# Attention: eight modulation blocks from TensorE to VectorE, loads in another order, results of two head pairs kept in h

## The chip, the cores and the metric

One core of a Trainium2 chip. The metric is the device time of one execution in microseconds (us). Engines are named as in the profile: PE (TensorE matmul), PEld (TensorE weight load), DVE (VectorE), ACT (ScalarE), POOL (GpSimd), SP (SyncE, which here only issues DMAs).

## The reference, cut to what matters

```python
def modulate(h, shift, scale):
    return h * (1 + scale) + shift
...
        sm, cm, gm, sf, cf, gf = adaln(c, w_ada[l], b_ada[l])    # silu(c) @ w_ada + b_ada, in six parts
        h = modulate(rmsnorm(x, norm_mix_g[l]), sm, cm)
            q, k, v = qkv_proj(h, w_qkv[j])
            o = neighbourhood_attention(q, k, v, cache_k[:, j], cache_v[:, j], rpb[j])
            mix = merge_heads(o) @ w_attn_out[j]
        x = x + gm * mix
        h = modulate(rmsnorm(x, norm_ffn_g[l]), sf, cf)
        x = x + gf * conv_ffn(h, ...)
```

Two layers, 1024 features, 16 heads of 64, 128 prompt tokens (conditioned by c_ctx) and 256 sample tokens (conditioned by c). Layer 0 mixes by attention, layer 1 by a gated MLP over chunks. In attention a prompt token sees the 128 prompt keys; a sample token sees the 256 sample keys within a window of columns, with a learned bias, and 128 cached keys. Everything is float32.

## The kernel before

Activations lie feature-major: x[k] holds 128 features of all 384 tokens. A float32 product is three products in a faster format, of operands split into a high part and a rest: hi·hi, hi·lo, lo·hi (`mac`, L101 to L105). Splitting a weight takes a cast on ACT (`hi`) and a subtraction on DVE (`lo`), L108 and L109. Weights come as tiles of 128 x 1024 (512 KB).

Attention (`attention`, L388) first makes V for all heads, then runs over eight pairs of heads (L597), with the keys of the next pair and the queries of the next pair made inside the pair; then come eight output products, one for each 128 features (`output`, L638), each followed by `residual` (L374). From L580 on the four engines PE, ACT, DVE and SP issue in the order in which the code is written (`tc.manual_schedule`); each engine runs its own list in order. What a pair's weights go through: `fetch` (L445) has SP load the next one into one of three buffers `st`; `ready` splits the oldest staged one and then calls `fetch`, so SP's next load waits until `lo` has read its buffer. `hi` and `lo` have five buffers each.

A pair t in the code before, in its order: scores of the sample's first 128 queries (and the prompt's); SP's loads of the next pair's cached keys (`cache`, tile kT) and bias (`bias_load`, two loads into btr); bias, minimum and exponentials (`exps`, L522: a DVE reduction that also adds the bias, then ACT's exponentials with their sums); transposes of the last pair's first head (`turn`); division by the sums (`normalized`, L540); the key product of the next pair; a `ready` (the *first lo*); scores of the second 128 queries; `keys` (khi on ACT, klo on DVE); `exps`, `turn`, `normalized` for them; the query product, a `ready` (the *second lo*), `bias`, `queries`, `values` of the last pair, and three steps of `ada`.

The modulations come from two places. `Ada` (L160) does blocks on PE: a block is 128 rows of w_ada for one of the parts gm, sf, cf of layer 0 (24 blocks, 512 KB each, buffers adw, four of them), L190; three are loaded and three are run in each pair. `AdaV` (L222) does the rest (56 blocks) on DVE in later stages: a block is 128 outputs of one part, multiplied by silu(c) and silu(c_ctx) (tiles cs, laid out over all partitions), each in one instruction that sums along the row (L248), and then the bias is added (L250).

Of the kernel before, what the change touches and what calls it, by code (L numbers as in the profile page):

```python
# [8 lines left out]
F32 = mybir.dt.float32  # L9
# [6 lines left out]
P = 128  # L16
D = 1024
# [22 lines left out]
def backbone(ctx: ExitStack, tc: tile.TileContext, xT_in, cond_in, condr_in, b_ada_in, prm_in,  # L40
# [17 lines left out]
    def bank(pool):  # L58
        return pool.tile([P, 512], F32, name="bank", tag="bank")
# [47 lines left out]
    def split(hi, lo, src):  # L107
        nc.scalar.copy(hi, src)  # L108
        nc.vector.tensor_tensor(lo, src, hi.bitcast(F32), ALU.subtract)  # L109
# [50 lines left out]
    class Ada:  # L160
# [1 line left out]


        def __init__(self):
            order = [(0, GM), (0, SF), (0, CF)]
            self.todo = [(l, pc, k) for l, pc in order for k in range(KD)]
            self.ready = []
            self.pa = self.done = None
# [9 lines left out]

        def run(self, n):
            for _ in range(n):  # L180
                if not self.ready:
                    self.load(1)
                self.one(*self.ready.pop(0))

        def one(self, l, pc, k, t):
            self.flush()
            if k == 0:
                self.pa = bank(ps_ad)
            for j in range(4):
                nc.tensor.matmul(self.pa[32 * j:32 * j + 32, 0:256], cond_s[:, k, :],  # L190
                                 t[:, 256 * j:256 * j + 256], start=(k == 0),
                                 stop=(k == KD - 1), tile_position=(0, 32 * j))
# [25 lines left out]
    class AdaV:  # L218


        def __init__(self):
            self.cs = self.junk = None  # L222

            def both(l, p, q):
                return [(l, pc, k) for k in range(KD) for pc in (p, q)]

            def one(l, p):
                return [(l, p, k) for k in range(KD)]

            self.todo = (both(1, SM, CM)[:8]  # L230
                         + [t for k in range(KD) for t in ((0, GF, k), both(1, SM, CM)[8 + k])]
                         + one(1, GM) + both(1, SF, CF) + one(1, GF))

        def start(self, pool):
            self.cs = [pool.tile([P, D], F32, name=f"cs{c}") for c in range(2)]
            self.junk = pool.tile([P, D], BF16, name="junk")
# [4 lines left out]
        def run(self, n):  # L241
            for _ in range(n):
                l, pc, k = self.todo.pop(0)
                t = adp.tile([P, D], F32, name="adw", tag="adw")
                nc.sync.dma_start(t, w_adaT[l, pc, k])
                m = mods[l][:, pc, k]
                for c in range(2):
                    tc.keep_in_program_order(nc.vector.tensor_tensor_reduce(  # L248
                        self.junk, t, self.cs[c], 1.0, 0.0, ALU.mult, ALU.add, m[:, c:c + 1]))
                nc.vector.tensor_scalar(m, m, b_ada[:, l, pc * 8 + k:pc * 8 + k + 1], None, ALU.add)  # L250
                if pc in (CM, CF):
                    gain(l, pc, slice(k, k + 1))

    ada_v = AdaV()

# [6 lines left out]
    def square(k, tag="t384", apart=True):  # L262

        sq["last"] = None
        if k == 0:
            sq["acc"] = tmp.tile([P, NT], F32, name="sqacc", tag="sqacc")
            nc.scalar.activation(sq["acc"], x[k], AF.Square)
            return
        t = tmp.tile([P, NT], F32, name="t384", tag=tag, bufs=2 if tag == "t384" else 1)
# [78 lines left out]
    def norm_first(nxt, units):  # L348

        w = [load(u) for u in units]  # L350
        Rp = rms()
        R = tmp.tile([P, NT], F32, name="R0", tag="R0")
# [35 lines left out]
    def attention(pool, wkp):  # L388
# [13 lines left out]
        ohi = [pool.tile([P, NT], F32R, name=f"ohi{t}") for t in range(NPAIR)]  # L402
        olo = [pool.tile([P, NT], F32R, name=f"olo{t}") for t in range(NPAIR)]
# [6 lines left out]
        R = tmp.tile([P, NT], F32, name="R0", tag="R0")  # L410
# [11 lines left out]
        for b in range(3):  # L422
            for half in range(2):
                nc.scalar.copy(V[:, b, 512 * half:512 * half + 512], acc[3 * half + b])
        nc.gpsimd.dma_start(sv_out, V[:, 0, :])

        allm = slice(0, P)

# [37 lines left out]
            return p  # L466

        def cache(t):
            kT = wkp.tile([P, 512], F32, name="kT", tag="kT", bufs=1)
            nc.sync.dma_start(kT[:, 256:384], ckT_in[:, t, :])  # L470
            return kT

        def keys(t, kT, p):
            nc.scalar.copy(kT[:, 0:256], p[:, 0:256])
            nc.scalar.copy(kT[:, 384:512], p[:, 256:384])  # L475
            nc.gpsimd.dma_start(skT_out[:, t, :], kT[:, 0:NPR])
            k = [wkp.tile([P, 512], F32R, name=n, tag=n) for n in ("khi", "klo")]
            split(*k, kT)
            return k

        def queries(p):
# [77 lines left out]
            nc.scalar.copy(pT[:, 512:896], two[1][:, :384])  # L559
            return pT  # L560

        def values(t, pT, pool=ps_mm):


            pv = bank(pool)
# [17 lines left out]
        for _ in range(3):  # L583
            fetch()
        kT, btr = cache(0), bias_load(0)
        nc.sync.dma_start(cv, cv_in)
        ada.load(3)
        ready()
        p = products()
        ready()  # L590
# [2 lines left out]
        ready()  # L593
        bias(btr)
        Q = queries(p)
        old = None
        for t in range(NPAIR):  # L597
            last = t == NPAIR - 1
# [17 lines left out]
            if last:  # L616
                ada.run(3)
            else:
# [5 lines left out]
            if not last:  # L624
                p = products()
                ready()
                bias(btr)
                Q = queries(p)
                if old is not None:
                    values(t - 1, pT)  # L630
                ada.run(3)
                ada.load(3)
                old = [(pr[hh], pc[hh]) for hh in range(2)]


        out = {}
# [17 lines left out]
        ready()  # L654
# [9 lines left out]
        for m in range(4, KD):  # L664
            output(m, range(KD), ps_mm if m % 2 else ps_sc)
            if m < KD - 2:
                ready()
            residual(0, GM, m, out[m][1], (0, SF, CF))


# [142 lines left out]
            residual(1, GM, m, ps, (1, SF, CF))  # L813


    with tc.tile_pool(name="att", bufs=1) as pool, tc.tile_pool(name="attw", bufs=2) as wkp:
        attention(pool, wkp)
    csp = ctx.enter_context(tc.tile_pool(name="cs", bufs=1))
    ada_v.start(csp)
# [97 lines left out]
```

## Time and profile before

| what | value |
|---|---|
| median of 3 runs | 1020.77 us (1020.12 to 1022.55) |
| profiled execution, time | 1021.07 us |
| its span | 1019.3 us |
| PE busy | 997.6 us (98%) |
| PEld busy | 947.1 us (93%) |
| DVE busy | 775.9 us (76%) |
| ACT busy | 482.0 us (47%) |
| DMA queue of SP (q1) | 170.11 MB, 51.8% of 16 engines |

The eight pairs take the stretch from about 74 to 190 us of the span, the output products end at 232 us, and the rest is the feed-forward and gated stages. In the profile's rows, "out<-in" names the tiles an instruction writes and reads, xN is a count, and an arrow to a releaser names what ended a wait. A busy engine's share is a mean over all stages.

### The profile page before, as it was taken

Reading aid. Unit: us, or ns where it says so; the run is one execution under the profiler, and the core shown is the slowest. Engines: PE = TensorE matmul, PEld = TensorE weight load, DVE = VectorE, ACT = ScalarE, POOL = GpSimd, SP = SyncE. Lnnn points to the kernel's source line nnn. Section 1 sums busy time; section 2 is a strip of 40 time slices with the busy share of each in tenths; the row PEclk is TensorE's granted clock in tenths of the full one; section 3 lists DMA queues with packets and bytes.
Section 4 is the critical chain, followed back from the end, with each engine's and each line's share of the span. In section 5 each row is a group of like instructions: output and inputs, shape, how many; then the busy total and the mean of one; then the engine's idle time right before and its main releaser. Section 6 shows DMA issues by size and latency. Waiting matters only on the chain.

```text
span 1019.3 us, 15937 instructions
## 1 busy us (share of the span) xinstructions
PE 997.6 (98%) x6012; PEld 947.1 (93%) x6012; DVE 775.9 (76%) x1591; ACT 482.0 (47%) x841; POOL 14.7 (1%) x29
## 2 busy tenths in 40 slices
PE   7999999999999999999999999999999999999996
PEld 6788788789999999999998889999999999999996
DVE  3646666568999898999989999688598777776652
ACT  3446555557655555433354434343385444443331
POOL 1000000000000000000000000000000000000000
PEclk7999999999999999999999999999999999999998
DMA  7874646624465555576737765565325434435521
GB/s 261 303 251 147 211 153 220 230 83 146 136 191 169 165 147 159 149 240 203 227 116 258 240 210 154 172 206 187 104 84 166 144 124 125 124 114 172 159 72 62
DMA packets 53933, 172.96 MB, mean 170 GB/s; under 512 B 6225, under 2 KB 12513, under 8 KB 53857
## 3 DMA queue, kind: packets, MB, share of 16 engines
q1 hardware_dynamic: 52992, 170.11, 51.8%
q8 instruction: 47, 0.77, 0.3%
q0 software_dynamic: 432, 1.06, 0.3%
q10 hardware_dynamic: 432, 0.79, 0.2%
q14 instruction: 30, 0.24, 0.1%
HBM read 169.31 MB, written 2.62 MB: 169 GB/s over the span
## 4 chain that ended last, share of the span: by engine, by line
PE 91%; DMA 3%; DVE 2%; ACT 2%; issue 1%; POOL 0%; SPq 0%; POOLq 0%; ACTq 0%; DVEq 0%
PE bank L103 28%; PE bank L105 28%; PE bank L104 28%; DMA kT<-in_ckT 2%; PE bank L145 1%; PE bank L788 1%; PE bank L568 1%; PE bank L519 1%; PE bank L190 1%; PE bank L551 1%; DMA adw<-in_w_ada 1%; PE bank L284 1%; ACT pr L536 0%; DMA cond<-in_cond 0%; PE bank L302 0%
## 5 line engine op out<-in xcount | busy, mean ns | idle before, releaser
L96 ACT CAST hi<-st 128x1024 fp32r<-128x1024 f32 (+1 forms) x192 | 198.1, 1033 | 300.6 <-PE bank L104 239.0
L105 PE MATMUL bank<-hhi,lo 128*128 128x384 f32 (+1 forms) x960 | 325.2, 339 | 0.2 <-DVE lo L109 0.2
L104 PE MATMUL bank<-hlo,hi 128*128 128x384 f32 (+1 forms) x960 | 324.7, 338 | 0.0
L103 PE MATMUL bank<-hhi,hi 128*128 128x384 f32 (+1 forms) x960 | 324.6, 338 | 0.0
L97 DVE TENSOR_TENSOR lo<-st,hi 128x1024 fp32r<-128x1024 f32 (+1 forms) x192 | 230.0, 1199 | 66.4 <-ACT hi L96 66.1
L105 PEld LDWEIGHTS bank<-hhi,lo 128*128 128x128 f32 x960 | 181.1, 189 | 0.5 <-DVE lo L109 0.5
L103 PEld LDWEIGHTS bank<-hhi,hi 128*128 128x128 f32 x960 | 181.0, 189 | 0.4 <-ACT kT L475 0.2
L104 PEld LDWEIGHTS bank<-hlo,hi 128*128 128x128 f32 x960 | 180.4, 188 | 0.1
L248 DVE CUSTOM_DVE_ANT_0 junk<-adw,cs 128x1024 bf16<-128x1024 f32 x112 | 136.6, 1219 | 1.0
L105 PE MATMUL bank<-ahi,lo 128*128 128x384 f32 x352 | 118.9, 338 | 0.0
L104 PE MATMUL bank<-alo,hi 128*128 128x384 f32 x352 | 118.9, 338 | 0.0
L103 PE MATMUL bank<-ahi,hi 128*128 128x384 f32 x352 | 118.7, 338 | 0.0
L105 PEld LDWEIGHTS bank<-ahi,lo 128*128 128x128 f32 x352 | 66.1, 188 | 0.0
L104 PEld LDWEIGHTS bank<-alo,hi 128*128 128x128 f32 x352 | 66.1, 188 | 0.0
L103 PEld LDWEIGHTS bank<-ahi,hi 128*128 128x128 f32 x352 | 66.1, 188 | 0.0
L103 PE MATMUL bank<-hi,hhi 128*128 128x512 f32 x144 | 58.2, 408 | 1.8 <-ACT hhi L330 1.8
L104 PE MATMUL bank<-lo,hhi 128*128 128x512 f32 x144 | 57.4, 398 | 0.0
L105 PE MATMUL bank<-hi,hlo 128*128 128x512 f32 x144 | 57.3, 399 | 0.0
L376 DVE SCALAR_TENSOR_TENSOR x<-bank,mod,x 128x128 f32<-128x128 f32 x64 | 23.8, 412 | 34.4 <-PE bank L105 34.2
L103 PE MATMUL bank<-mhi,hi 128*128 128x384 f32 x128 | 43.3, 339 | 0.0
L105 PE MATMUL bank<-mhi,lo 128*128 128x384 f32 x128 | 43.2, 337 | 0.0
L104 PE MATMUL bank<-mlo,hi 128*128 128x384 f32 x128 | 43.1, 337 | 0.0
(154 smaller groups left out, 1265.5 us busy)
## 6 DMA issues: line engine op xcount, KB each, us to landing
st<-in_w_up SPq DMA_DIRECT2D x88, 512.0 KB, 3.6
adw<-in_w_adaT SPq DMA_DIRECT2D x56, 512.0 KB, 4.2
adw<-in_w_ada SPq DMA_DIRECT2D x40, 512.0 KB, 5.6
st<-in_w_down SPq DMA_DIRECT2D x32, 512.0 KB, 3.6
st<-in_w_qk SPq DMA_DIRECT2D x16, 512.0 KB, 3.7
st<-in_w_gu SPq DMA_DIRECT2D x16, 512.0 KB, 4.3
st<-in_w_gv SPq DMA_DIRECT2D x16, 512.0 KB, 4.5
st<-in_w_gout SPq DMA_DIRECT2D x16, 512.0 KB, 4.5
```

The source lines that it names most:

```text
L96: nc.scalar.copy(hi[:, :n], st[:, :n])
L97: nc.vector.tensor_tensor(lo[:, :n], st[:, :n], hi[:, :n].bitcast(F32), ALU.subtract)
L103: nc.tensor.matmul(out, a[0], b[0], start=start, stop=False)
L104: nc.tensor.matmul(out, a[0], b[1], start=False, stop=False)
L105: nc.tensor.matmul(out, a[1], b[0], start=False, stop=stop)
L145: nc.tensor.matmul(pa[32 * j:32 * j + 32, 0:P], cond_s[:, 4 * hf + kk, :], w[hf][:, kk, P * q:P * q + P], start=(kk == 0), stop=(kk == 3), ...
L190: nc.tensor.matmul(self.pa[32 * j:32 * j + 32, 0:256], cond_s[:, k, :], t[:, 256 * j:256 * j + 256], start=(k == 0), stop=(k == KD - 1), t ...
L248: tc.keep_in_program_order(nc.vector.tensor_tensor_reduce(self.junk, t, self.cs[c], 1.0, 0.0, ALU.mult, ALU.add, m[:, c:c + 1]))
L284: mm = nc.tensor.matmul(ss[:, 2 * b:2 * b + 2], src[:, b * P:(b + 1) * P], ones[:, 0:2], start=(i == 0 and b == 0), stop=(i == len(srcs) - ...
L376: nc.vector.scalar_tensor_tensor(x[m][:, a:b], ps[:, a:b], mod(l, gate, m, c), x[m][:, a:b], ALU.mult, ALU.add)
L519: nc.tensor.matmul(sc[hh][:, cols], q[qp][HS[hh], qs:qs + P], k[kp][HS[hh], ks], start=i == 0, stop=i == 2)
L551: nc.tensor.transpose((ta[:, o:o + P] if g < 2 else tb[:, o - 512:o - 512 + P]), pr[:, b, g * P:g * P + P], ident)
```

## The change

What it does, by parts:

- The eight blocks of gm move from `Ada` to `AdaV`, first in its list. In the attention loop `AdaV`'s step is cut in three: `load` (SP), `half(0)` for the prompt, `half(1)` for the sample and the bias. One block is done in each pair. `Ada` keeps 16 blocks: two are run ahead of the loop and two in each pair up to the seventh.
- cs is loaded and silu taken ahead of the pairs, no longer after attention; the throw-away output of the sums lies in a buffer of tmp during attention.
- The loads of cached keys and bias are issued at the end of a pair, for the pair after the next, ahead of the blocks.
- Cached keys go to a tile of their own (ck), and the keys are split in three pieces from ck and from the product's bank, without the copy to kT; a copy for the output state (sk) is made afterwards.
- `bias` comes ahead of the second `normalized`.
- The results ohi, olo of pairs 6 and 7 lie in columns of hhi and hlo, which hold h until the last query product.
- The end: the last pair stops after its second `exps`; the order of outputs, `values` 6 and 7, transposes and residuals changes, whole outputs 3 to 7 go to five banks, and residuals come three outputs later.

On SP, in the middle of the loop, the loads before (st: weights, adw<-in_w_ada: blocks for PE, kT: cached keys, btr: bias):

```order
L450 DMA st<-in_w_qk 128x1024 x2
L176 DMA adw<-in_w_ada 128x1024 x3
L470 DMA kT<-in_ckT 128x128
L499 DMA btr<-in_rpb 64x2x219 x2
L450 DMA st<-in_w_o 128x1024 x2
```

and now (adw<-in_w_adaT: the block for DVE, ck: cached keys):

```order
L458 DMA st<-in_w_qk 128x1024 x2
L478 DMA ck<-in_ckT 128x128
L509 DMA btr<-in_rpb 64x2x219 x2
L241 DMA adw<-in_w_adaT 128x1024
L176 DMA adw<-in_w_ada 128x1024 x2
L458 DMA st<-in_w_o 128x1024 x2
```

Of the two weights in a row, the first is let go by the first lo and the second by the second lo. Keys and bias moved ahead of the blocks, DVE's block stands behind them, and one block for PE is gone.

On DVE in the same pairs, from the reductions of the first half to the second lo, before:

```order
L533 TENSOR_REDUCE st<-bank 128x1 x2
L541 RECIPROCAL st<-st 128x4
L543 TENSOR_SCALAR pr<-pr,st 128x384 x2
L543 TENSOR_SCALAR pc<-pc,st 128x128 x2
L109 TENSOR_TENSOR lo<-st,hi 128x1024
L109 TENSOR_TENSOR klo<-kT,khi 128x512
L526 ISA bank,st<-bank,bt 128x384
...
L541 RECIPROCAL st<-st 128x2
L543 TENSOR_SCALAR pr<-pr,st 128x384 x2
L109 TENSOR_TENSOR lo<-st,hi 128x1024
L509 TENSOR_TENSOR bt<-mask,btr 128x3x128 x2
L485 SCALAR_TENSOR_TENSOR qlo<-bank,qhi 128x384
```

and now (L246 is the half of a block, L249 its bias):

```order
L543 TENSOR_REDUCE st<-bank 128x1 x2
L246 ISA junk,mod_143<-adw,cs_718 128x1024
...
L551 RECIPROCAL st<-st 128x4
...
L109 TENSOR_TENSOR lo<-st,hi 128x1024
L109 TENSOR_TENSOR klo<-ck,khi 128x128
L109 TENSOR_TENSOR klo<-bank,khi 128x256
...
L519 TENSOR_TENSOR bt<-mask,btr 128x3x128 x2
L551 RECIPROCAL st<-st 128x2
L553 TENSOR_SCALAR pr<-pr,st 128x384 x2
L246 ISA junk,mod_143<-adw,cs_719 128x1024
...
L249 TENSOR_SCALAR mod_143<-mod_143,b_ada 128x2
L109 TENSOR_TENSOR lo<-st,hi 128x1024
```

Half 0 went between the reductions and the first reciprocal, half 1 between the second division and the second lo, the bias moved up, and klo became three pieces (two are shown).

On PE in the last pair, after the second scores, before (ohi: results of pairs as left operand, one row of three shown for a product):

```order
L519 MATMUL bank<-khi,qlo 128x384 x2
L190 MATMUL bank<-adw,cond_s 32x256 x12
L551 MATMUL bank<-ident,pr 128x128 x6
L553 MATMUL bank<-ident,pc 128x128
L103 MATMUL bank<-ohi_177,hi 128x384
```

and now:

```order
L529 MATMUL bank<-khi,qlo 128x384 x2
L103 MATMUL bank<-ohi_180,hi 128x384
...
L103 MATMUL bank<-ohi_185,hi 128x384
...
L561 MATMUL bank<-ident,pr 128x128 x6
L563 MATMUL bank<-ident,pc 128x128
```

The three blocks are gone, and the first output product over pairs 0 to 5 stands ahead of the transposes.

The diff, cut:

```diff
@@ class Ada
-            order = [(0, GM), (0, SF), (0, CF)]
+            order = [(0, SF), (0, CF)]
@@ class AdaV
-            self.todo = (both(1, SM, CM)[:8]
+            self.todo = (one(0, GM) + both(1, SM, CM)[:8]
...
+        def load(self):
+            l, pc, k = self.todo.pop(0)
+            t = adp.tile([P, D], F32, name="adw", tag="adw")
+            nc.sync.dma_start(t, w_adaT[l, pc, k])
+            return l, pc, k, t
+
+        def half(self, c, l, pc, k, t):
+            m = mods[l][:, pc, k]
+            tc.keep_in_program_order(nc.vector.tensor_tensor_reduce(
+                self.junk, t, self.cs[c], 1.0, 0.0, ALU.mult, ALU.add, m[:, c:c + 1]))
+            if c:
                 nc.vector.tensor_scalar(m, m, b_ada[:, l, pc * 8 + k:pc * 8 + k + 1], None, ALU.add)
@@ attention
+        ohi = [pool.tile([P, NT], F32R, name=f"ohi{t}") for t in range(6)] + [hhi[:, t, :NT] for t in (6, 7)]
+        olo = [pool.tile([P, NT], F32R, name=f"olo{t}") for t in range(6)] + [hlo[:, t, :NT] for t in (6, 7)]
...
+        ada_v.start(csp, tmp.tile([P, D], BF16, name="junk", tag="R0"))
...
-            nc.scalar.copy(kT[:, 0:256], p[:, 0:256])
-            nc.scalar.copy(kT[:, 384:512], p[:, 256:384])
             k = [wkp.tile([P, 512], F32R, name=n, tag=n) for n in ("khi", "klo")]
-            split(*k, kT)
+            for o, src in ((256, ck), (0, p[:, 0:256]), (384, p[:, 256:384])):
+                s = slice(o, o + src.shape[1])
+                split(k[0][:, s], k[1][:, s], src)
...
         kT, btr = cache(0), bias_load(0)
+        ada.load(2)
+        block = ada_v.load()
         nc.sync.dma_start(cv, cv_in)
-        ada.load(3)
...
+        kT, btr = cache(1), bias_load(1)
+        ada.run(2)
+        ada.load(2)
         old = None
         for t in range(NPAIR):
...
-            if not last:
-                kT, btr = cache(t + 1), bias_load(t + 1)
             e = exps(0, sc, pr, pc)
+            ada_v.half(0, *block)
...
             e = exps(1, sc, pr, pc)
+            if last:
+                break
             if old is not None:
                 pT.append(turned(1, turn(*old[1])))
+            bias(btr)
             normalized(*e)
+            ada_v.half(1, *block)
+            p = products()
+            ready()
+            Q = queries(p)
+            ada.flush()
+            if old is not None:
+                values(t - 1, pT)
+            if t < NPAIR - 2:
+                kT, btr = cache(t + 2), bias_load(t + 2)
+            ada.run(2)
+            block = ada_v.load()
+            ada.load(2)
...
         output(0, range(6), ps_mm)
+        pT.append(turned(1, turn(*old[1])))
+        normalized(*e)
         ready()
-        values(6, pT, ps_sc)
+        pv = bank(ps_sc)
         output(1, range(6), ps_sc)
+        ada.flush()
+        values(6, pT, pv)
         ready()
+        ada_v.half(1, *block)
         pT = [turned(0, turn(pr[0], pc[0]))]
         output(0, (6,))
         output(1, (6,))
         pT.append(turned(1, turn(pr[1], pc[1])))
-        output(2, range(7), ps_mm)
-        ready()
+        output(2, range(5), ps_mm)
         values(7, pT)
-        output(3, range(7), ps_sc)
-        ada.flush()
-        for m in range(4):
+        output(2, (5, 6))
+        for m in range(3):
             output(m, (7,))
-            residual(0, GM, m, out[m][1], (0, SF, CF))
-            if m == 1:
+        for m in range(3, KD):
+            output(m, range(KD), (ps_sc, ps_ta, ps_ad, ps_mm, ps_sc)[m - 3])
+            if m < KD - 1:
                 ready()
+            residual(0, GM, m - 3, out[m - 3][1], (0, SF, CF))
         order.__exit__(None, None, None)
```

More of the change, by code (lines that the diff above doesn't have):

```diff
@@ L180, in run @@
             for _ in range(n):
-                if not self.ready:
-                    self.load(1)
                 self.one(*self.ready.pop(0))
         def one(self, l, pc, k, t):
-            self.flush()
             if k == 0:
@@ L228, in one, with start @@
                 return [(l, p, k) for k in range(KD)]
-            self.todo = (both(1, SM, CM)[:8]
+            self.todo = (one(0, GM) + both(1, SM, CM)[:8]
                          + [t for k in range(KD) for t in ((0, GF, k), both(1, SM, CM)[8 + k])]
                          + one(1, GM) + both(1, SF, CF) + one(1, GF))
-        def start(self, pool):
+        def start(self, pool, junk):
+            self.junk = junk
             self.cs = [pool.tile([P, D], F32, name=f"cs{c}") for c in range(2)]
-            self.junk = pool.tile([P, D], BF16, name="junk")
             for c in range(2):
@@ L239, in start @@
                 nc.scalar.activation(self.cs[c], self.cs[c], AF.Silu)
[L241 to L249, printed above, removed]
+        def load(self):
[8 more added lines that the diff above has]
+            if c:
                 nc.vector.tensor_scalar(m, m, b_ada[:, l, pc * 8 + k:pc * 8 + k + 1], None, ALU.add)
@@ L252, in run @@
                     gain(l, pc, slice(k, k + 1))
+        def run(self, n):
+            for _ in range(n):
+                block = self.load()
+                for c in range(2):
+                    self.half(c, *block)
     ada_v = AdaV()
@@ L268, in square @@
             return
-        t = tmp.tile([P, NT], F32, name="t384", tag=tag, bufs=2 if tag == "t384" else 1)
+        t = tmp.tile([P, NT if tag == "t384" else 512], F32, name="t384", tag=tag,
+                     bufs=2 if tag == "t384" else 1)[:, :NT]
         nc.scalar.activation(t, x[k], AF.Square)
@@ L351, in norm_first @@
         Rp = rms()
-        R = tmp.tile([P, NT], F32, name="R0", tag="R0")
+        R = tmp.tile([P, 512], F32, name="R0", tag="R0")[:, :NT]
         nc.scalar.copy(R, Rp[:, :NT])
@@ L401, in attention @@
         cv = pool.tile([P, D], F32, name="cv")
-        ohi = [pool.tile([P, NT], F32R, name=f"ohi{t}") for t in range(NPAIR)]
-        olo = [pool.tile([P, NT], F32R, name=f"olo{t}") for t in range(NPAIR)]
+        ohi = [pool.tile([P, NT], F32R, name=f"ohi{t}") for t in range(6)] + [hhi[:, t, :NT] for t in (6, 7)]
+        olo = [pool.tile([P, NT], F32R, name=f"olo{t}") for t in range(6)] + [hlo[:, t, :NT] for t in (6, 7)]
         for k in range(KD):
@@ L409, in attention @@
         Rp = rms(ss, True)
[L410 removed]
+        R = tmp.tile([P, 512], F32, name="R0", tag="R0")[:, :NT]
         nc.scalar.copy(R, Rp[:, :NT])
@@ L468, in cache, with keys @@
         def cache(t):
[L469 to L473, printed above, removed]
-            nc.scalar.copy(kT[:, 0:256], p[:, 0:256])
-            nc.scalar.copy(kT[:, 384:512], p[:, 256:384])
-            nc.gpsimd.dma_start(skT_out[:, t, :], kT[:, 0:NPR])
-            k = [wkp.tile([P, 512], F32R, name=n, tag=n) for n in ("khi", "klo")]
-            split(*k, kT)
+            ck = wkp.tile([P, P], F32, name="ck", tag="ck", bufs=1)
+            nc.sync.dma_start(ck, ckT_in[:, t, :])
+            return ck
+        def keys(t, ck, p):
+            k = [wkp.tile([P, 512], F32R, name=n, tag=n) for n in ("khi", "klo")]
+            for o, src in ((256, ck), (0, p[:, 0:256]), (384, p[:, 256:384])):
+                s = slice(o, o + src.shape[1])
+                split(k[0][:, s], k[1][:, s], src)
+            sk = wkp.tile([P, NPR], F32, name="sk", tag="sk", bufs=1)
+            nc.scalar.copy(sk, p[:, 0:NPR])
+            nc.gpsimd.dma_start(skT_out[:, t, :], sk)
             return k
@@ L560, in turned, with values @@
             return pT
-        def values(t, pT, pool=ps_mm):
-            pv = bank(pool)
+        def values(t, pT, pv=None):
+            pv = bank(ps_mm) if pv is None else pv
             def part(hh, cols, vv, o, n, start, stop):
@@ L615, in attention @@
             scores(1, Q, K, sc)
-            if last:
-                ada.run(3)
-            else:
+            if not last:
                 K = keys(t + 1, kT, p)
             e = exps(1, sc, pr, pc)
+            if last:
+                break
             if old is not None:
                 pT.append(turned(1, turn(*old[1])))
+            bias(btr)
             normalized(*e)
-            if not last:
-                p = products()
-                ready()
[L627 to L633, printed above, removed]
+            ada_v.half(1, *block)
[10 more added lines that the diff above has]
+            ada.load(2)
+            old = [(pr[hh], pc[hh]) for hh in range(2)]
         out = {}
@@ L652, in attention @@
         pT.append(turned(1, turn(pr[1], pc[1])))
-        output(2, range(7), ps_mm)
-        ready()
+        output(2, range(5), ps_mm)
         values(7, pT)
-        output(3, range(7), ps_sc)
-        ada.flush()
-        for m in range(4):
+        output(2, (5, 6))
+        for m in range(3):
             output(m, (7,))
-            residual(0, GM, m, out[m][1], (0, SF, CF))
-            if m == 1:
+        for m in range(3, KD):
+            output(m, range(KD), (ps_sc, ps_ta, ps_ad, ps_mm, ps_sc)[m - 3])
+            if m < KD - 1:
                 ready()
+            residual(0, GM, m - 3, out[m - 3][1], (0, SF, CF))
         order.__exit__(None, None, None)
[L664 to L667, printed above, removed]
+        for m in range(KD - 3, KD):
             residual(0, GM, m, out[m][1], (0, SF, CF))
@@ L813, in gmlp @@
             residual(1, GM, m, ps, (1, SF, CF))
+    csp = ctx.enter_context(tc.tile_pool(name="cs", bufs=1))
     with tc.tile_pool(name="att", bufs=1) as pool, tc.tile_pool(name="attw", bufs=2) as wkp:
         attention(pool, wkp)
-    csp = ctx.enter_context(tc.tile_pool(name="cs", bufs=1))
-    ada_v.start(csp)
+    ada_v.junk = csp.tile([P, D], BF16, name="junk")
     with tc.tile_pool(name="ffn0", bufs=1) as pool, tc.tile_pool(name="ffn0w", bufs=2) as wkp:
```

## The prediction

> **What bounds the kernel now.** I read the page first, then the chain of waits inside the attention loop, then SP's waits, then the groups of VectorE's instructions there, and last single transfers. All times are in the profiled execution (span 1019.3 us, time 1021.07, 0.3 above the median of 1020.77). Two rows of the page:
>
> ```profile
> PE 997.6 (98%) x6012; PEld 947.1 (93%) x6012; DVE 775.9 (76%) x1591; ACT 482.0 (47%) x841; POOL 14.7 (1%) x29
> PE 91%; DMA 3%; DVE 2%; ACT 2%; issue 1%; POOL 0%; SPq 0%; POOLq 0%; ACTq 0%; DVEq 0%
> ```
>
> PE looks like the bound, but the share is modelled and is a mean over stages. The chain that ends one head pair (134 to 150 us) is not PE's:
>
> ```profile
> 136.52 7.56 DMA kT<-in_ckT
> 144.16 0.63 ACT khi L108
> 144.81 0.69 DVE klo L109
> 145.50 0.47 DVE bank L526
> 146.07 1.24 ACT pr L536 x4
> ...
> 148.16 0.95 ACT hi L108
> ```
>
> The 64 KB of cached keys are issued at 136.52, behind a 512 KB weight and three 512 KB blocks, and land at 144.08; khi, klo, the softmax of the second half and the split of the second weight follow, and that split frees SP's next load:
>
> ```profile
> SPq L450 <- DVE lo L109: 58.5, 10, 7.8
> ```
>
> SP waited 58.5 us of these 80 for lo. So the pair is a closed loop: second lo ends, SP issues, transfers land, VectorE works, next second lo ends. I call that end L2. The thirteen splits between 84 and 183 us are the first pair's second and two for each of six pairs:
>
> ```profile
> L109 DVE TENSOR_TENSOR lo<-st,hi x13: 1224/1225/1226, 84.7 to 180.8; 128x1024 fp32r<-128x1024 f32 x13
> ```
>
> L2 of pair 0 is 84.7+1.2 = 85.9, that of pair 6 is 182.0: six periods of 16.0 us. Busy times of stretches (start to end, length, then PE, PEld, DVE, ACT, POOL busy with instruction counts):
>
> ```profile
> 101.97:182.01 80.04, 77.90 (x602) 65.41 (x598) 49.47 (x132) 45.23 (x121) 2.69 (x5) 1.00 0.55 187
> 134.64:150.37 15.73, 15.66 (x128) 13.49 (x124) 9.78 (x27) 8.83 (x23) 0.54 (x1) 1.00 0.54 191
> 182.01:232.22 50.21, 45.97 (x316) 41.16 (x309) 31.47 (x74) 27.32 (x60) 0.00 (x0) 1.00 0.49 169
> ```
>
> Five pairs hold 77.9 us of PE, 15.6 each; VectorE has 9.9 of 16, so there is room on it, but whether at the right moment is the question.
>
> **The change part by part.** *Blocks taken off PE.* Three blocks cost PE
>
> ```profile
> 181.62 1.48 PE bank L190 x24
> ```
>
> 0.5 us a block. PE's floor of a pair becomes 15.6 - 0.5 = 15.1. But the loop above is not PE's, so this by itself buys nothing until the loop is shorter.
>
> *The halves on VectorE.* Half 0 now stands ahead of the reciprocal, half 1 ahead of the second lo. VectorE is in order, and half 0's block is issued only after L2 of the pair before: weight, cached keys, two bias loads, then the block. While it waits, reciprocal, the first lo, klo and all the second half are queued behind it; PE waits for the first lo in its second product. So the old loop through kT goes and one through the block takes its place. Let H be the start of half 0 and x = H - L2. The work from H to the next L2 is from these groups (mean ns ahead of the idle time; window 103 to 183, the last three from later in the kernel, same shapes):
>
> ```profile
> L109 DVE TENSOR_TENSOR lo<-st,hi 128x1024 fp32r<-128x1024 f32 x10 | 12.3, 1225 | 6.5 <-ACT hi L108 6.5
> L526 DVE CUSTOM_DVE_ANT_0 bank<-bank,bt 128x384 f32<-128x384 f32 x20 | 10.8, 580 | 1.9 <-PE bank L519 1.8
> L543 DVE TENSOR_SCALAR pr<-pr,st 128x384 f32<-128x384 f32 x20 | 7.5, 418 | 0.4
> L509 DVE TENSOR_TENSOR bt<-mask,btr 128x384 f32<-128x384 f32 x10 | 5.1, 552 | 0.0
> L543 DVE TENSOR_SCALAR pc<-pc,st 128x128 f32<-128x128 f32 x10 | 2.4, 281 | 0.0
> L541 DVE RECIPROCAL st<-st 128x4 f32<-128x4 f32 (+1 forms) x10 | 1.7, 172 | 13.0 <-ACT pc L536 9.1 <-ACT pr L536 4.0
> ...
> L248 DVE CUSTOM_DVE_ANT_0 junk<-adw,cs 128x1024 bf16<-128x1024 f32 x112 | 136.6, 1219 | 1.0
> L250 DVE TENSOR_SCALAR mod<-mod,b_ada 128x2 f32<-128x2 f32 x55 | 12.2, 222 | 0.4
> L248 DVE DVE_READ_ACCUMULATOR2_ANT mod<- 128x1 f32 x111 | 9.1, 82 | 0.0
> ```
>
> Neighbours overlap by almost 0.1 us (the chain counts 0.47 for a 0.58 L526), so: half 0 1.14; reciprocal, two pr, two pc 1.27; lo 1.14; klo in three pieces 0.74 instead of 0.69; two L526 1.0 and two L509 0.95, the latter now inside the wait for the exponentials; reciprocal and two pr 0.88; half 1 and its addition 1.4; lo 1.22. Sum 9.74. The period is 9.74 + x, against 16.0: it breaks even at x = 6.3.
>
> *What x is.* No row shows this order in the loop, so I bound it by the nearest transfers (times of issue, then time to landing): the loop's weights; two groups at the start, at 72.9 and at 56.1; the three blocks of the last pair and those of the pair at 135, with queue 8's packets from 134.6 to 144.1 and, last, in the whole kernel:
>
> ```profile
> L450 SPq DMA_DIRECT2D st<-in_w_qk x6: 333/334/334, 110.5 to 150.4; - x6
> ...
> DMA to landing us min/median/max: 3.3/3.5/3.9
> ...
> L450 SPq DMA_DIRECT2D st<-in_w_qk x1: 328/328/328, 72.9 to 72.9; - x1
> L499 SPq DMA_DIRECT2D btr<-in_rpb x2: 601/604/607, 73.8 to 74.5; - x2
> DMA to landing us min/median/max: 3.7/3.8/3.8
> ...
> L450 SPq DMA_DIRECT2D st<-in_w_qk x1: 328/328/328, 56.1 to 56.1; - x1
> L586 SPq DMA_DIRECT2D cv<-in_cv x1: 593/593/593, 58.4 to 58.4; - x1
> DMA to landing us min/median/max: 5.1/5.1/5.1
> ...
> L176 SPq DMA_DIRECT2D adw<-in_w_ada x3: 382/382/383, 182.5 to 183.4; - x3
> DMA to landing us min/median/max: 4.4/5.2/6.0
> ...
> L176 SPq DMA_DIRECT2D adw<-in_w_ada x3: 381/382/384, 135.1 to 136.0; - x3
> DMA to landing us min/median/max: 4.2/5.1/7.8
> q8 instruction: 1, 0.02, 0.6%
> ...
> q8 instruction: 47, 0.77, 0.3%
> ```
>
> SP needs 74.5 - 72.9 + 0.66 = 2.28 us from the weight's issue to the block's. Landing 3.4 after that (weights, 512 KB with little in front, took 3.3 to 3.9 in the loop, the first group) gives x = 5.7, the lower end. The second bias load of the 72.9 group ended at 74.5+3.8 = 78.3, 5.4 after the weight; another 512 KB in a burst adds 1.3 (182.5+4.4, 182.9+5.2, 183.4+6.0 land 1.3 apart): x = 6.7. The 56.1 group has exactly the new order, weight, keys, bias twice, 512 KB: cv landed at 58.4+5.1 = 63.5, x = 7.4, but behind leftovers. I take 6.45, between the two without leftovers (6.2, a burst that fills the engines, and 6.7).
>
> To that comes a lag. The same three loads took 6.0 when nothing else moved and 7.8 when one 16 KB packet of queue 8, instructions, came in their midst (the row for 134.6 to 144.1): 1.8 us. The page has 47 such packets for PE's 12,024 matmuls and weight loads, one in 256. A pair now has 128 + 124 = 252, so the packet keeps its place in the pair; with 16 fewer it comes about 1 us later in each and leaves the 4.4 us in which the block is under way. I count two lags in the six pairs, bounds none and six. [...]
>
> *Start.* Two blocks on PE ahead of pair 0 (1.0 us) lie in the existing wait for the weights; half 1 in pair 0 costs 1.4 plus small pieces, so L2(0) moves from 85.9 to 87.65. From there L2(1) = 87.65 + x + 9.74 = 97.39 + x against 101.97: x - 4.6. Moving the 1 MB of cs ahead of the first head weights delays those by up to 2 x 1.3 = 2.6 us; PE then still has V's products to do, so I take 0, and 2.6 as the upper end.
>
> *Five pairs:* 5 (9.74 + x - 16.0) = 5x - 31.3.
>
> *The end of attention.* Before, L2(6) to the end of the output products is 50.2 us, two stalls among them:
>
> ```profile
> 183.42 6.02 DMA adw<-in_w_ada
> PE bank L103 <- DVE x L376: 1.9, 1, 1.9
> L105 PE MATMUL bank<-ohi,lo x64: 334/337/343, 191.2 to 232.1; 128*128 128x384 f32 x64
> ```
>
> PE idled 50.2 - 46.0 = 4.2 there, mostly for three blocks in the last pair and for banks after the first residuals (1.9), and the blocks cost it 1.5 more. All that goes, 5.7. By steps: in the last pair no keys or bias are in front of the block: it comes right after the weight, as the 182.5 load, 4.4 + 0.5 = 4.9. From H of pair 7: lo of w_o at 3.6 (half 0 to lo above), its six-block output and the transposes to 9.5, the split of values 6 awaited there, then PE in line: 16.9 where it waits for the last values, 18.5, and five whole outputs of 4.2: 39.5. Together 44.4 against 50.2: -5.8. Squares and residuals 5 to 7 follow in the next stage as before; I take 0 after attention, where cs no longer loads.
>
> *Sum:* (x - 4.6) + (5x - 31.3) - 5.8 = 6x - 41.7; x = 6.45 gives -3.0, two lags +3.6: +0.6, forecast 1020.77 + 0.6 = 1021.4 us. The measurement can tell 0.3%, 3.06 us: the mean x with lags has to be under 6.44 for a clear gain and over 7.46 for a clear loss; mine is 7.05.
>
> **Rivals.** *The block is hidden, faster.* Transfers overlap, SP's issue alone counts: x = 5.7, no lag: -7.5, 1013.3; PE's floor of 15.1 a pair stops it at x = 5.36, -9.5, 1011.3. For it: VectorE idles there for the exponentials anyway (9.1 us in five pairs at L541, more than five halves of 1.14), and bias loads have few bytes. Against: they landed 0.8 us apart, so they are not free. [...]
>
> *The block is later, slower.* x is the 7.4 of cv's group: +2.7, and with two lags +6.3, 1027.1. It decides once the mean x passes 7.46. For it: that group is the only one in the new order. Against: it had other loads in front.
>
> *The tail doesn't gain.* The wait for w_o's lo and the bank chain over five pools replace both stalls: +5.8, 1026.6. Against: the units are one ahead, and residuals lag three outputs.
>
> **How the numbers follow.** Forecast 0.38, hidden 0.33, later 0.20, tail 0.05, rest 0.04. Faster 0.35 (hidden, half of the rest), same 0.38, slower 0.27 (later, tail, half of the rest). The range goes from between the hidden case's two ends, 1012, to the later case with one more part of a lag, 1028; the forecast's own is 1018 to 1024.
>
> **What would show it.** In the changed profile: VectorE idle ahead of the L246 half 0 for a DMA of adw, some 2 to 4 us in each pair, and SP no longer behind kT; PE waiting for the first lo in its second product, 1 to 2 us (period less 15.1); L2 to L2 near 16.2 to 16.8; no PE wait for adw in the last pair. I am wrong if half 0 starts straight after the reductions, or if PE no longer waits in the loop.

## The result and the profile after

The changed kernel takes 1030.46 us (median of 4, 1029.51 to 1032.82) beside 1021.66 before (median of 4): ratio 1.0096, 95% interval 1.0075 to 1.0116. The forecast was no measurable change, 1021.4, with a range to 1028: it is slower than that. The profiled execution has a span of 1028.3 us, 9.0 above the one before. The page:

```profile
PE 994.4 (97%) x5946; PEld 945.2 (92%) x5946; DVE 795.0 (77%) x1646; ACT 478.1 (46%) x848; POOL 14.7 (1%) x29
PE 86%; DVE 6%; DMA 4%; SPq 1%; issue 1%; ACT 1%; POOL 1%; POOLq 0%; ACTq 0%; DVEq 0%
L246 DVE CUSTOM_DVE_ANT_0 junk<-adw,cs 128x1024 bf16<-128x1024 f32 x128 | 156.1, 1219 | 29.7 <-DMA adw<-in_w_adaT 28.7
```

PE is busy 3.2 us less, and the chain now runs through it for 86% of the span, not 91%. The third row names the new wait: the halves (L246; L248 before, where they had 1.0 us of idle time ahead of them) stood 28.7 us for their blocks. The thirteen splits from the second lo of pair 0 to that of pair 6 and the waits of DVE and PE in the loop (us in total, times, longest), then busy times of the loop and of the end of attention (the third number from the end is PE's granted clock):

```profile
L109 DVE TENSOR_TENSOR lo<-st,hi x13: 1214/1219/1221, 86.2 to 193.9; 128x1024 fp32r<-128x1024 f32 x13
DVE junk L246 <- DMA adw<-in_w_adaT: 26.7, 6, 5.7
DVE klo L109 <- ACT khi L108: 2.0, 6, 0.3
PE bank L105 <- DVE lo L109: 15.2, 6, 3.7
...
87.40:195.10 107.70, 91.95 (x670) 78.27 (x670) 72.51 (x196) 52.87 (x148) 3.24 (x6) 0.97 0.53 167
195.10:239.84 44.74, 43.52 (x280) 40.37 (x273) 31.47 (x75) 25.92 (x59) 0.00 (x0) 1.00 0.44 153
```

Six periods take 193.9 - 86.2 = 107.7, 17.95 each instead of 16.0. PE waits 15.2 us for lo, which stands in DVE's queue behind the half that waits for its block. PE's clock was 0.97 in the loop, because it was 0.51 and 0.50 in two stretches of 3.4 us, from 98.5 and from 153.2 us on; from half 0 to the next second lo's end all six pairs took 10.1 us, those two as well, so the clock lengthened none of them. The chain of one pair shows the loop closed, as foreseen, but wider:

```profile
158.14 1.23 DVE lo L109
...
160.28 0.61 SPq L509
...
160.94 0.60 SPq L509
...
161.63 5.40 DMA adw<-in_w_adaT
...
167.06 1.23 DVE junk L246
...
169.56 1.15 DVE lo L109
```

From the end of the second lo, 159.37, to half 0 at 167.06 x is 7.69. In the six pairs it was 7.81, 7.36, 7.58, 8.77, 7.70 and 7.82, mean 7.84.

### The profile page after: what moved, and what is told of

It reads as the page before. It is cut to its first block, busy times and chain, and to the rows that moved or that the text cites. A ratio compares the mean times of both kernels' runs of the same rounds, so it can differ in the third digit from the quotient of the medians.

```text
span 1028.3 us, 15842 instructions
## 1 busy us (share of the span) xinstructions
PE 994.4 (97%) x5946; PEld 945.2 (92%) x5946; DVE 795.0 (77%) x1646; ACT 478.1 (46%) x848; POOL 14.7 (1%) x29
## 4 chain that ended last, share of the span: by engine, by line
PE 86%; DVE 6%; DMA 4%; SPq 1%; issue 1%; ACT 1%; POOL 1%; POOLq 0%; ACTq 0%; DVEq 0%
PE bank L105 27%; PE bank L103 27%; PE bank L104 27%; DMA adw<-in_w_adaT 4%; DVE junk L246 1%; DVE lo L109 1%; PE bank L807 1%; PE bank L145 1%; PE bank L578 1%; DMA adw<-in_w_ada 1%; DVE pr L553 1%; POOL ry L319 1%; DVE bank L536 0%; PE bank L529 0%; PE bank L308 0%
## 5 line engine op out<-in xcount | busy, mean ns | idle before, releaser
L105 PE MATMUL bank<-hhi,lo 128*128 128x384 f32 (+1 forms) x976 | 332.0, 341 | 15.4 <-DVE lo L109 15.4
L104 PE MATMUL bank<-hlo,hi 128*128 128x384 f32 (+1 forms) x976 | 331.6, 340 | 0.1
L103 PE MATMUL bank<-hhi,hi 128*128 128x384 f32 (+1 forms) x976 | 331.4, 340 | 0.0
L105 PEld LDWEIGHTS bank<-hhi,lo 128*128 128x128 f32 x976 | 185.1, 190 | 18.1 <-DVE lo L109 17.7
L103 PEld LDWEIGHTS bank<-hhi,hi 128*128 128x128 f32 x976 | 184.9, 189 | 0.6 <-ACT khi L108 0.2
L104 PEld LDWEIGHTS bank<-hlo,hi 128*128 128x128 f32 x976 | 184.5, 189 | 0.6 <-DVE hlo L109 0.3
L246 DVE CUSTOM_DVE_ANT_0 junk<-adw,cs 128x1024 bf16<-128x1024 f32 x128 | 156.1, 1219 | 29.7 <-DMA adw<-in_w_adaT 28.7
L103 PE MATMUL bank<-ahi,hi 128*128 128x384 f32 x352 | 118.7, 338 | 0.0
L103 PEld LDWEIGHTS bank<-ahi,hi 128*128 128x128 f32 x352 | 66.1, 188 | 0.0
L103 PE MATMUL bank<-hi,hhi 128*128 128x512 f32 x144 | 58.2, 408 | 1.8 <-ACT hhi L336 1.8
L103 PE MATMUL bank<-mhi,hi 128*128 128x384 f32 x128 | 43.3, 339 | 0.0
```

The costliest lines, as they stand in the source:

```text
L103: nc.tensor.matmul(out, a[0], b[0], start=start, stop=False)
L104: nc.tensor.matmul(out, a[0], b[1], start=False, stop=False)
L105: nc.tensor.matmul(out, a[1], b[0], start=False, stop=stop)
L246: tc.keep_in_program_order(nc.vector.tensor_tensor_reduce(self.junk, t, self.cs[c], 1.0, 0.0, ALU.mult, ALU.add, m[:, c:c + 1]))
```

## Experiments

The theory: half 0 waits on DVE for its block; the bias loads (and less the keys) in front hold the block back; everything behind half 0, the first lo above all, is passed the wait. The main rival: DVE's longer list, or another part of the change, costs the time. Times are medians; "before" ran on the same chip beside each (1021.23, 1020.33 and 1021.09 in the three groups). Executions of one kernel spread by up to 8 us (before: 1017.0 to 1024.7 in the second group), and a profiled execution lies up to 2.4 us from its median. The changed kernel was timed once, beside a before of 1021.66, so differences from it carry about 1 us more of doubt than the ratios to before.

**The block ahead of keys and bias.**

```diff
+            block = ada_v.load()
             if t < NPAIR - 2:
                 kT, btr = cache(t + 2), bias_load(t + 2)
             ada.run(2)
-            block = ada_v.load()
             ada.load(2)
```

> Edit: at the end of a pair the block for VectorE is loaded ahead of the cached keys and the bias; nothing else. Theory (half 0 waits for its block, which the two bias loads in front of it hold back): x, from the second lo's end to half 0, falls from 7.8 (mean of the changed kernel) to 4.9, as the blocks right behind a weight land now; the pair to the larger of 10.1 + 4.9 = 15.0 and PE's 15.1, so 6 x (17.95 - 15.1) = 17 less: about 1013 us. Rival (the transfers share the engines whatever the order, and the keys or the bias, now later, hold up klo or the bias addition): x stays over 7 or a new VectorE wait for ck or btr of 2 us and more; time within 3 us of 1030.

Measured 1017.19, ratio to before 0.9962 (0.9949 to 0.9975); 13 less than the changed kernel, and 4 above the expected 1013. The splits of lo, the block's load at two places with its time to landing, and PE's wait:

```profile
L109 DVE TENSOR_TENSOR lo<-st,hi x13: 1215/1218/1220, 85.9 to 178.5; 128x1024 fp32r<-128x1024 f32 x13
L241 SPq DMA_DIRECT2D adw<-in_w_adaT x1: 384/384/384, 87.6 to 87.6; - x1
DMA to landing us min/median/max: 4.6/4.6/4.6
...
L241 SPq DMA_DIRECT2D adw<-in_w_adaT x1: 1492/1492/1492, 102.7 to 102.7; - x1
DMA to landing us min/median/max: 6.3/6.3/6.3
...
PE bank L105 <- DVE lo L109: 2.9, 4, 1.9
```

The pair is (178.5 - 85.9)/6 = 15.4, which is the work of 10.1 and a mean x of 5.3; x is 4.9 to 5.2 in five pairs and 6.75 in one. In that one the load's issue took SP 1.49 us instead of 0.38, when a packet of queue 8 moved (102.9; kind "instruction", 16 KB, 47 of them on the page of the changed kernel). No new wait for keys or bias shows. One line of order thus turns the loss into a gain.

**Only the bias behind the block.**

```diff
             if t < NPAIR - 2:
-                kT, btr = cache(t + 2), bias_load(t + 2)
-            ada.run(2)
+                kT = cache(t + 2)
             block = ada_v.load()
+            if t < NPAIR - 2:
+                btr = bias_load(t + 2)
+            ada.run(2)
             ada.load(2)
```

> Edit: order weight, cached keys, block, bias twice, two blocks for PE. Tells whether the keys (64 KB in rows of 512 B) or the bias (219 KB in rows of 876 B) hold the block back. Theory that it is the bias: x = 4.9 plus 0.3 for the keys, 5.2; pair 15.3; about 1014 to 1015 us. Theory that any small rows in front cost alike, or SP's issue: x near 6.5, pair 16.6, about 1022.

Measured 1018.95, ratio 0.9980 (0.9968 to 0.9992).

```profile
L109 DVE TENSOR_TENSOR lo<-st,hi x13: 1217/1220/1222, 86.7 to 184.4; 128x1024 fp32r<-128x1024 f32 x13
```

A pair of 16.3 and a mean x of 6.16, between the two expectations (5.2 and 6.5). So of the 2.5 us between the block in front (5.31 in the mean) and the changed order (7.84) the bias makes 1.7. The 0.85 for the keys, more than I gave them, is not certain: three of the six stretches held a packet of queue 8 (x 7.04, 6.95, 6.38); of those without, one has 6.06 and two have 5.2 and 5.3. By the stretches without a packet alone (means of 5.0, 5.5 and 7.8) the bias makes 2.2 and the keys 0.5. The bias is the larger part either way.

**The block a pair ahead.**

```diff
-ADA_BUFS = 4
+ADA_BUFS = 3
...
+        coming_v = ada_v.load(wkp)
...
             ada.run(2)
-            block = ada_v.load()
+            block = coming_v
+            if t < NPAIR - 2:
+                coming_v = ada_v.load(wkp)
             ada.load(2)
```

> Edit: the order of loads stays, but the block is loaded a whole pair ahead into buffers of its own (the pool adw has three buffers instead of four, the small tile st of exps two instead of four, to make room). Theory: half 0 starts right after the reductions (x near 2.8), VectorE's loop is 12.9, and PE's 15.1 a pair bounds: about 1013, the same as with the block first; PE waits for lo below 0.3 us a pair. Rival (VectorE's longer list itself holds PE up, not the wait for the load): pair 16 or more, 1019 and over. The three buffers may cost up to 2 us in later stages.

Measured 1009.91, ratio 0.9903 (0.9880 to 0.9926): the best of all, 11 us below before, and a version that beats both kernels. Splits, and busy times over five pairs:

```profile
L109 DVE TENSOR_TENSOR lo<-st,hi x13: 1217/1220/1227, 88.5 to 176.1; 128x1024 fp32r<-128x1024 f32 x13
103.75:177.15 73.40, 73.40 (x566) 63.32 (x562) 61.46 (x165) 44.06 (x125) 2.70 (x5) 1.00 0.66 211
```

PE is busy in all of 73.4 us: with one block less a pair needs no more than 14.6 to 14.7, which I take as PE's floor, lower than the 15.1 that I had. DVE does the same list as in the changed kernel, so the rival that its length costs the time falls.

**Half 0 behind the first lo, loads as in the change.**

```diff
             e = exps(0, sc, pr, pc)
-            ada_v.half(0, *block)
...
             ready()
+            ada_v.half(0, *block)
             sc = [bank(ps_mm if last else ps_sc) for _ in range(2)]
```

> Edit: order of loads as in the changed kernel, half 0 moved on VectorE from ahead of the reciprocal to behind the first lo. Theory (in-order waiting, not the transfer as such, is what costs): the first lo is ready 5 us after the second, PE's second product no longer waits, half 0 waits to 7.8 and the loop is 7.8 + 10.1 - 2.4 = 15.5: about 1016. Rival (the block's lateness is passed on in full wherever half 0 stands): 1027 and over.

Measured 1018.71, ratio 0.9984 (0.9967 to 1.0002).

```profile
L109 DVE TENSOR_TENSOR lo<-st,hi x13: 1217/1221/1226, 88.5 to 184.3; 128x1024 fp32r<-128x1024 f32 x13
PE bank L529 <- DVE qlo L495: 2.8, 4, 2.0
```

The pair is 16.0: 2 us less with the loads as late as ever (the block landed 7.7 to 8.5 us after the second lo's end). What cost was what stood behind the wait in DVE's order. Why the pair is half a microsecond above the 15.5 expected is not separated; DVE waits 10.8 us for exponentials over these pairs.

**The gm blocks back on PE, the rest of the change kept.**

```diff
-            order = [(0, SF), (0, CF)]
+            order = [(0, GM), (0, SF), (0, CF)]
...
-            ada_v.half(0, *block)
...
-            ada_v.half(1, *block)
...
-            ada.run(2)
-            block = ada_v.load()
-            ada.load(2)
+            ada.run(3)
+            ada.load(3)
```

> Edit: the changed kernel with the gm blocks back on PE (three blocks a pair, three ahead of the loop, no halves in the loop); order of small loads, keys in pieces, cs, results in h and the end stay. Theory (only the wait of half 0 costs, the rest of the change gains): PE bounds with 14.7 (measured with the block a pair ahead) + 0.5 = 15.2 a pair, 6 x (17.95 - 15.2) = 16.5 less than the changed kernel: about 1014, some 7 below before. Rival (keys in pieces, cs ahead or the new end cost too): 1018 and over.

Measured 1012.00, ratio 0.9911 (0.9879 to 0.9942).

```profile
L109 DVE TENSOR_TENSOR lo<-st,hi x13: 1224/1226/1227, 83.5 to 174.5; 128x1024 fp32r<-128x1024 f32 x13
```

A pair of 15.2, as expected. The other parts of the change together are worth 9 us, and the move of the eight blocks, with its loads in this order, costs 18. How the 9 divide among the small loads ahead, the keys in pieces, cs and the end is not shown.

**The kernel before with the small loads ahead, alone.**

```diff
-            if not last:
-                kT, btr = cache(t + 1), bias_load(t + 1)
...
+                if t < NPAIR - 2:
+                    kT, btr = cache(t + 2), bias_load(t + 2)
                 ada.run(3)
                 ada.load(3)
```

> Edit: the kernel before with one part of the change alone: cached keys and bias are loaded at the end of a pair, ahead of PE's three blocks, for the pair after the next. Theory (before was bound by the loop through kT, which landed 9.4 us after the second lo): kT lands 3.8 us after it, klo waits for nothing, the pair falls from 16.0 to PE's 15.2: six pairs, 4 to 5 less, about 1016.5. Rival (before was PE's, the loop only looked like it): within 1.5 us of before.

Measured 1018.47, ratio 0.9972 (0.9956 to 0.9988), 2 above the expected 1016.5. Splits, PE's wait for blocks in the end of attention, busy times of that end, and two stretches of it:

```profile
L109 DVE TENSOR_TENSOR lo<-st,hi x13: 1224/1225/1227, 83.5 to 175.1; 128x1024 fp32r<-128x1024 f32 x13
PE bank L190 <- DMA adw<-in_w_ada: 2.6, 3, 1.8
176.36:230.85 54.49, 50.02 (x329) 44.80 (x326) 31.57 (x74) 28.10 (x60) 0.00 (x0) 0.94 0.48 160
185.30:188.70 3.40, 3.40 (x20) 3.02 (x13) 2.45 (x8) 2.72 (x8) 0.00 (x0) 0.50 0.89 281
212.60:216.00 3.40, 3.40 (x13) 3.40 (x12) 2.84 (x7) 3.40 (x7) 0.00 (x0) 0.51 0.00 0
```

The pair fell from 16.0 to 15.3, as the loop through kT required, 4.4 us over six. In the profiled execution the end of attention took back 4: 54.5 against 50.2. The blocks are not the reason, since PE waits 2.6 us for them here and waited 2.4 before. PE's granted clock is: it was 0.50 and 0.51 in two stretches of 3.4 us, with PE busy all the time, where it was 1.00 before, and PE's busy time in the end grew from 46.0 to 50.0; by an estimate from these shares the two stretches cost 3.4 us. What lowered the clock is not shown. The fastest other execution, 1016.11, had the highest mean clock, 0.994 against 0.990 in this one, and lies at the expectation.

**The bias loaded twice.**

```diff
-            for rr in range(2):
+            for tile_ in ((btr, wkp.tile(..., name="btr2")) if t else (btr,)):
+                for rr in range(2):
```

> Edit: the changed kernel with each pair's two bias loads done twice, the second time into a tile that nobody reads. Prices the bias rows (256 rows of 876 B in two loads). Theory that the bias in front holds the block back by their own time on the engines (about 1.5 us) or SP's issue (1.3 us): x grows by 1.3 to 2 a pair, 8 to 12 more: 1038 to 1042. Rival (bias overlaps with the weight, no cost): within 3 us of 1030.

Measured 1040.45, ratio 1.0183 (1.0142 to 1.0225). Splits of pairs 0 to 5:

```profile
L109 DVE TENSOR_TENSOR lo<-st,hi x11: 1218/1220/1221, 86.8 to 183.9; 128x1024 fp32r<-128x1024 f32 x11
```

A pair of (183.9 - 86.8)/5 = 19.4; with the sixth pair the mean is 19.6. Over the six, x grew by 1.6 to a mean of 9.46 (8.8 to 10.3). The bias in front costs its own time, at the price expected.

**Block in front and half 0 behind the first lo.**

```diff
-            ada_v.half(0, *block)
...
             ready()
+            ada_v.half(0, *block)
...
+            block = ada_v.load()
             if t < NPAIR - 2:
                 kT, btr = cache(t + 2), bias_load(t + 2)
             ada.run(2)
-            block = ada_v.load()
```

> Edit: block loaded ahead of keys and bias and half 0 behind the first lo, both with no more memory. Theory: the block is there 2 us before VectorE wants it, nothing waits for it, PE's 14.7 a pair bounds: as with the block a pair ahead, 1010 us. Rival (half 0 in the new place delays klo, and with it the second half of the pair, so VectorE's loop bounds): the pair near 15.5 to 16, 1015 to 1018.

Measured 1014.96, ratio 0.9940 (0.9921 to 0.9960): between the two expectations, with the rival's pair.

```profile
L109 DVE TENSOR_TENSOR lo<-st,hi x13: 1217/1221/1227, 86.5 to 179.0; 128x1024 fp32r<-128x1024 f32 x13
DVE st L551 <- ACT pc L546: 10.8, 6, 1.8
PE bank L529 <- DVE qlo L495: 3.0, 5, 2.0
```

No wait for a block is left, and yet the pair is 15.4. DVE idles up to 1.8 us a pair for the exponentials (10.8 in six), and then the half stands on the way to klo; PE waits for qlo. With the block a pair ahead the half fills that idle time, and the pair is 14.6. The place between reductions and reciprocal is the right one, for a block that is there.

**The bias loads cut short.** This kernel leaves out most of the bias of pairs 1 to 7 and uses that of pair 0 for all.

```diff
-            btr = wkp.tile([P, 2, 219], ...)
+            n = 8 if t else 219
+            b = wkp.tile([P, 2, n], ...)
...
-                            [[1, 64], [465, 2], [1, 219]]))
+                            [[1, 64], [465, 2], [1, n]]))
```

> Edit: the changed kernel with the bias loads of pairs 1 to 7 cut from 219 to 8 elements a row (pair 0's bias is used for all pairs); as many issues in the same places. Tells SP's issue time from the rows' own time. If the rows of 876 B hold the block back (256 rows of near 95 ns on 16 engines, 1.5 us): x falls from 7.8 to about 6.3, the pair to 16.4, about 1021. If it is the 1.3 us that SP takes to issue the two loads: x stays within 0.4 of 7.8, about 1029.

Measured 1022.80, ratio 1.0028 (1.0011 to 1.0045).

```profile
L109 DVE TENSOR_TENSOR lo<-st,hi x13: 1214/1220/1221, 85.3 to 186.3; 128x1024 fp32r<-128x1024 f32 x13
```

The pair is 16.8 and x 6.7 in the mean, 1.1 less, with as many issues: two thirds of the bias's price (1.7) are its rows. The 256 rows that are left, of 32 B, held a DMA engine 8 ns each, 0.13 us over 16 engines by an estimate, so I put most of the other third down to SP's two issues (0.6 us each in the changed kernel); that was not tried by itself.

**The old order of the end.** Outputs 0 to 3 up to seven pairs, then residuals behind each, as before; the last division and half 1 ahead of the first output.

```diff
-            if last:
-                break
...
+            if last:
+                ada.flush()
+                break
...
+        for m in range(4):
             output(m, (7,))
+            residual(0, GM, m, out[m][1], (0, SF, CF))
```

> Edit: the changed kernel with the old order of the end (last pair with transposes and division ahead of the first output, outputs in banks of two pools, residuals right after their outputs; only residuals 6 and 7 come after the last output, since their results share memory with pairs 6 and 7). Prices the new end. Theory (the sum: 5.8 for the whole end, of which the blocks that left PE 1.5 and their wait 2.4 stay gained): about 2 more than the changed kernel, 1032.5, with the 1.9 wait for the first residuals back. Rival (the new order gave nothing): within 1 us of 1030.5.

Measured 1039.63, ratio 1.0196 (1.0171 to 1.0221): 9 slower than the changed kernel, where 2 were expected. PE's waits from 185 us on, and a stretch of the end:

```profile
PE bank L203 <- ACT pT L569: 4.0, 1, 4.0
PE bank L105 <- DVE lo L109: 2.8, 1, 2.8
PE bank L561 <- ACT pT L568: 2.2, 1, 2.2
PE bank L103 <- DVE x L382: 1.9, 1, 1.9
201.20:211.30 10.10, 6.12 (x22) 5.72 (x21) 6.16 (x16) 3.66 (x8) 0.00 (x0) 0.50 0.48 142
```

The 1.9 for the first residuals is back as expected; the 2.8 still belongs to the loop. The 2.2 and the 4.0 are waits for copies of transposes (pT), which stand behind the exponentials of their half in ACT's order and, in this order, ahead of the first output in PE's (the 4.0 at the flush of PE's modulations, which this edit put behind those copies). The block was not late for them: half 0 of the last pair waited 0.4 us for it. Besides, PE's granted clock was 0.50 for ten microseconds with 6.1 us of PE's work in them, some 3 us lost by an estimate from that share; in the changed kernel it was 1.00 in the end. So this run doesn't price the new end by itself. It shows that the new end's early first output gives PE work during the last pair's softmax, where in the changed kernel half 0 also waits 2.0 us for its block.

## Why the prediction was wrong

*What bounded the kernel:* right. Small loads ahead shortened the loop by 0.7 a pair without any other edit, and PE's busy share of 98% would have denied it.

*The mechanism:* right. DVE waits in order for the block, the first lo and PE behind it (15.2 us of PE's waits in the loop name it), klo no longer waits for cached keys (its 2.0 us over six pairs are for a cast on ACT), and no block is waited for by PE in the last pair.

*The term that failed is x.* "I take 6.45, between the two without leftovers"; measured 7.84. The row in the same order, cv's group with 7.4, was the one to take: 7.36 to 7.82 came in five of six pairs, with nothing left over. I had set it aside for its leftovers, although the weight ahead of cv had landed after 3.8 us, within the loop's 3.3 to 3.9, so that they had hardly held it up; that the two values agree so closely may still be luck in part. I pieced the value together from a bias load with no large transfer behind it, plus 1.3 for a block. The pieces don't add. In the changed kernel the same weight, keys and bias, with the block queued behind, landed as follows (issue, time to landing):

```profile
L458 SPq DMA_DIRECT2D st<-in_w_qk x1: 328/328/328, 159.4 to 159.4; - x1
DMA to landing us min/median/max: 3.6/3.6/3.6
L509 SPq DMA_DIRECT2D btr<-in_rpb x2: 602/604/607, 160.3 to 160.9; - x2
DMA to landing us min/median/max: 3.9/4.3/4.7
L241 SPq DMA_DIRECT2D adw<-in_w_adaT x1: 543/543/543, 161.6 to 161.6; - x1
DMA to landing us min/median/max: 5.4/5.4/5.4
```

The second bias load took 4.7 instead of 3.8, and only then, 1.4 later, came the block. With x = 7.84 instead of 6.45 and two lags (a mean of 7.05), six pairs cost 4.7 more. The rival "the block is later" (7.4, a mean of 8.0 with two lags, 1027.1; it decides past a mean of 7.46) was the case that came; I gave it 0.20 against 0.38. The rival "the block is hidden" (5.7) fell furthest short.

*The lag:* over-sized. Three of the six stretches held a packet of queue 8, and one was longer by 1.1 us (8.77); in the other two the lengthened issue (1.50 and 1.29 us) fell on PE's blocks behind it (usual: 0.38 to 0.42). Without any lag x would have been 7.65. The packets did not keep one place in the pair: behind L2 of pairs 1 to 5 they came 3.1, 3.4, 4.8, 9.2 and 12.5 us. The 1.8 had been read from 7.8 against 6.0 as the packet's doing alone; but from 103 us on every third block of the loop before took 7.8 to 8.4, each with a packet near it and with keys and bias behind it, so the two were never told apart.

*From H to L2:* 9.74 foreseen, 10.11 measured. The rows of DVE over the six pairs:

```profile
L109 DVE TENSOR_TENSOR klo<-bank,khi 128x256 fp32r<-128x256 f32 x6 | 2.5, 417 | 0.0
L109 DVE TENSOR_TENSOR klo<-bank,khi 128x128 fp32r<-128x128 f32 x6 | 1.8, 292 | 2.0 <-ACT khi L108 2.0
L109 DVE TENSOR_TENSOR klo<-ck,khi 128x128 fp32r<-128x128 f32 x6 | 1.7, 285 | 0.0
```

Klo in three pieces was taken as 0.74 and took 1.16: the third waits 0.33 for its cast on ACT, a wait that the sum had put at nothing. Six times the 0.37 is 2.2.

*The rest:* the start was 0.25 better than said. The end of attention, -5.8 foreseen, is 44.7 against 50.2, -5.5. After attention 1.4 were lost where I had put 0. PE's waits from 238 to 265 us, of which there were none in the same place before, have one row:

```profile
PE bank L308 <- DVE rr L324: 0.6, 1, 0.6
```

It is the norm's inverse, and three residuals now come after the last output ahead of it; that these cause it is argued, not tried. What the other 0.8 is stays open. Together, with 0.3 lost at the end and 0.3 won at the start: 4.7 + 2.2 + 1.4 + 0.3 - 0.3 = 8.3 of the 8.4 between +0.6 and +9.0; x makes more than half of it, and without its error the time would have lain within the range.

*PE's floor,* 15.1, was too high: 14.7. With the gm blocks back on PE, and so with the work of before, a pair took 15.2, where PE's busy time in the rows before was 15.6; that these rows held time stretched by waits is argued from this. The hidden case's end was therefore lower than its 1011.3: the block a pair ahead reached 1009.9.

## What to carry to other kernels

Before work is put into an idle stretch of an in-order engine, ask when its data lands, counted from the event that lets its load go, and what is queued behind it on that engine; here one load issued 1.9 us earlier, or a pair ahead, moved the kernel by 13 and 20 us. "Small loads first" holds for the load that is waited for: loads that nobody needs soon go behind it, even small ones (here two bias loads of 110 KB in front of it cost 1.7 us a pair). Where one row shows transfers in the very order that is to come, take it over a value put together from others. And before a loss in a stage is put down to its waits, the granted clock there is worth a look: in two of these runs it was 0.50 for 7 and 10 us, by the estimates above 3 to 4 us of their time.

## What the runs showed of the hardware

A bias load in rows of 876 B is no small transfer. 219 KB of them in front of the block cost as much as a 512 KB block does behind another (1.6 by the doubled bias, 1.7 by the exchange, against 1.3): in the trace's packets between 159.5 and 167.2 a row of 876 B held its DMA engine 99 ns in the mean (56 in the median), one of 4096 B 171 ns (159). The price is not the row's alone: in the kernel before, between 134.6 and 144.1, the same rows held it 48 ns (41), the long ones 179 (159). By the means, a byte of the bias cost 2.7 times one of the long rows in the changed kernel and 1.2 times in the kernel before. What makes the difference between the two places is not shown.

A packet of queue 8 that moves while SP issues a load can go with a longer issue: 1.5 us instead of 0.4 at 102.7 with the block in front, where the block landed 6.3 us after its issue began instead of 4.6, and 1.5 and 1.3 us in the changed kernel (108.3 and 126.2; the packets began at 108.4 and 126.1). Not every packet does it: five later ones of the changed kernel's run began during an issue that took the usual 0.33 us.

The split operands' format was the faster one: in the kernel before, products of plain float32 with 128 columns (vn by ws, L788) began 112 ns apart in the median, products of split operands with 384 columns (ahi by hi, L103) 175 ns.
